# Layer 0's experts in order of their token counts, ten alone and six in pairs, rows fetched from DRAM

## Chip, cores and metric

One core of a Trainium2 chip (trn2). The metric is the device time of one execution in microseconds (us); smaller is better. All times are of this one core.

## What is computed

A two-layer block (mixer, then a mixture of experts, MoE) followed by a second block. Layer 0's mixer is a Fourier and neighbourhood attention mixer, layer 1's is retention. The change is in layer 0's MoE, which takes 512 tokens (256 of the context, 256 of the sequence) of 1024 numbers and 16 experts:

```python
def moe_ffn(tok, router_w, router_b, w1, w3, w2):
    T = tok.shape[0]
    scores = jax.nn.sigmoid((tok @ router_w).astype(jnp.float32))
    biased = (scores + router_b.astype(jnp.float32)).reshape(T, N_GROUPS, EXPERTS_PER_GROUP)
    group_score = lax.top_k(biased, TOP_K)[0].sum(axis=-1)
    g_sel = jnp.argmax(group_score, axis=-1)
    in_group = jnp.take_along_axis(biased, g_sel[:, None, None], axis=1)[:, 0]
    _, local = lax.top_k(in_group, TOP_K)
    expert_idx = g_sel[:, None] * EXPERTS_PER_GROUP + local
    w = jnp.take_along_axis(scores, expert_idx, axis=-1)
    w = w / jnp.sum(w, axis=-1, keepdims=True)
    gate = ...
    for e in range(N_EXPERTS):
        hid = jax.nn.silu(tok @ w1[e]) * (tok @ w3[e])
        out = out + gate[:, e:e + 1] * (hid @ w2[e])
```

Each token goes to two of four experts in one group. w1 and w3 of an expert are 1024 x 512, w2 is 512 x 1024, all float32: 6 MB per expert, 96 MB per layer. The kernel never computes all 512 tokens for an expert; it collects the tokens that chose it, up to 128 places.

## The kernel before, in words

**Engines.** PE multiplies, PEld loads its weights, DVE and ACT and POOL do elementwise work, SP issues the loads. Each takes its instructions in order. The program is written as if in sequence; a scheduler orders each engine's instructions before the run.

**Float32 products in three passes.** `unit` (L191) loads 1 MB of weights and splits it in two halves of 128 x 1024: ACT writes the high part `wh` (L202), DVE the rest `wl` (L205), and POOL every fourth `wl` where `pool_every=4`. The split tiles have four buffers each. `mm3` then makes three matmuls: high by high, low by high, high by low (L214 to L216).

**Layer 0, `moe` (L1044).** `route` (L944) normalizes the tokens, finds each token's experts and gates, and its `rows` writes the tokens' rows to SBUF as `nat`, a high and a low half. `places` numbers the tokens of each expert. A one-hot matrix `oh` (`choose`, L1086) says which token holds which place, and `gather` (L1110) multiplies it with both halves of `nat`: this gives `xe`, the tokens of two experts with features on partitions. The loop goes over the experts in their fixed order, two to a one-hot. For each: w1's product, `silu`, one gather step of the next two experts, w3's product, the product of both, another gather step, then w2 of the expert before (`second`), then four transposes of the hidden layer. `slots` (L1094) multiplies the one-hot with gates and token numbers, so that DVE can compute which DRAM row a place belongs to (L1097 to L1101).

`second` scales the result by the gate. Experts 0 to 13 add it to `fD` in DRAM by an indirect DMA on POOL's queue (L1149); experts 14 and 15 stay on the chip and are put back by a matmul with a one-hot `back` (L1155, L1156) after the loop, where `fD` is read as `comb` and added to the residual.

**Overflow.** `overflow` (L1443), called in the second expert, reads a count into registers and branches (L1466): if an expert has more than 128 tokens, a loop over all experts serves the rest. Every engine passes that branch.

**Buffers.** Weights rotate through three raw buffers of 1 MB and two more of `moe`; SP issues each load when its buffer is free. Each weight load of layer 0 has runs of 2 KB, since row `k*128+p` goes to partition `p`. Part of layer 1's adaLN product (`ada`, L395) is put between the steps of the start by `fill`.

**Layer 1, `moe_late` (L1217), 256 tokens.** Its experts 0 to 13 are ranked on the chip by their counts, and 14 and 15 stay first in place (`NS = 2`). Two of them alone, then seven pairs that share PE's 128 columns (L1374); weights are used in float32 as loaded, in runs of 8 KB (partition `p` holds rows `8p` to `8p+7`), from an expert number that SP reads into a register. `GROUPS` gives the ranks and the places of each group, `caps` the places of each rank, and a token beyond them is the overflow's.

Of the kernel before, what the change touches and what calls it, by code (L numbers as in the profile page):

```python
# [18 lines left out]
P = 128  # L19
# [20 lines left out]
GROUPS = (((15, 128),), ((14, 128),), ((0, 96), (13, 32)), ((1, 96), (12, 32)), ((2, 64), (11, 64)),  # L40
          ((3, 64), (10, 64)), ((4, 64), (9, 64)), ((5, 64), (8, 64)), ((6, 64), (7, 64)))
BATCHES = ((0, 1), (2, 3), (4, 5), (6, 7), (8,))
CAPS = [dict(x for g in GROUPS for x in g)[r] for r in range(16)]


def host_constants():
# [13 lines left out]
    r = np.zeros((P, 44), f)  # L60
# [5 lines left out]
    r[:, 28:44] = CAPS  # L66
# [60 lines left out]
class Kern:  # L127
# [63 lines left out]
    def unit(self, w, kc0, c0, nk=8, ncol=256, pool_every=0):  # L191

        nc = self.nc
        src = w[kc0 * P:(kc0 + nk) * P, c0:c0 + ncol].rearrange("(k p) c -> p k c", p=P)
        t = self.raw((P, nk, ncol), src)
# [136 lines left out]
    def setup_late(self, pool):  # L332
        nc, I, cp, V = self.nc, self.I, self.cp, self.nc.vector
        row = lambda ap, p=P: ap.rearrange("(r p) -> r p", p=p)
        cr = cp.tile([P, 44], F32, name="c_route")
        nc.sync.dma_start(out=cr, in_=I["c_route"])
        self.wg4 = cr[:, 0:4]
        self.down16, self.caps = cr[:, 4:20], cr[:, 28:44]
# [605 lines left out]
    def route(self, l, ss, rp, spread):  # L944
# [69 lines left out]
        nat = [rp.tile([P, NT, D], F32R, tag=f"nat{i}", name=self.name("nat")) for i in range(2)]  # L1014

        def rows():
            for k in range(KC):
# [12 lines left out]
                if spread:  # L1030
                    w = P // KC
                    dst = [x.rearrange("p t (m q) -> p t q m", m=KC)[:, :, w * k:w * k + w, :] for x in nat]
                    self.split_evac(dst, tp.rearrange("p t (q m) -> p t q m", m=KC))
                else:
                    parts = self.split_evac([x[:, :, k * P:(k + 1) * P] for x in nat], tp)
                    if k == HK[0] and self.holds:
                        self.holds[0] = parts
                    if k == HK[1] and self.holds:
                        self.holds[1:] = [parts]
# [4 lines left out]
    def moe(self, ss):  # L1044
        nc, I, V = self.nc, self.I, self.nc.vector
        l, n0, NT, N = 0, 0, 4, 512
        with ExitStack() as es:
# [4 lines left out]
            self.aside.append(self.ada(1, 0, lambda i: wp.tile([P, 2048], F32, tag=f"xe{i % 2}", name=self.name("ada"))))  # L1052
            self.fill(2)
            tl, places, gates, rows, nat = self.route(l, ss, rp, False)
            rows()
            pos, posm = places()
            cnt = tl([2])
            V.tensor_reduce(out=cnt[:, 0:1], in_=pos[:, 4, :], axis=AX.X, op=OP.max)
            g, den = gates()

            pk = tl([16, NT, 4])
            pe = pk.rearrange("p e t c -> p t e c")
            V.tensor_tensor(out=pe[:, :, :, 3], in0=g, in1=den, op=OP.mult)
            nc.gpsimd.tensor_copy(pe[:, :, :, 0], posm)
            for t in range(NT):
                nc.gpsimd.tensor_copy(pe[:, t, :, 1:3], self.tokm[:, t].unsqueeze(1).to_broadcast([P, 16, 2]))

            pr4 = tl([16, NT, 4], F32R)
            nc.gpsimd.tensor_copy(pr4[:, :, :, 0:3], pk[:, :, :, 1:4])
            nc.gpsimd.tensor_tensor(out=pr4[:, :, :, 3:4], in0=pk[:, :, :, 3:4], in1=pr4[:, :, :, 2:3].bitcast(F32),  # L1070
                                    op=OP.subtract)
            iota = tl([N], F32, "iota")
            nc.gpsimd.iota(iota, pattern=[[1, N]], base=0, channel_multiplier=0, allow_small_or_imprecise_dtypes=True)
            idx = tl([16], I32, "idx")
            fidx = tl([16])
            gate = tl([16])

            direct = range(14, 16)

            def choose(p):  # L1080


                oh = wp.tile([P, NT, 256], F32R, tag="oh", name=self.name("oh"))
                for t in range(NT):
                    for e in range(2):
                        V.tensor_scalar(out=oh[:, t, e * P:(e + 1) * P], in0=self.iota1,  # L1086
                                        scalar1=posm[:, t, 2 * p + e:2 * p + e + 1], scalar2=None, op0=OP.is_equal)
                return oh

            def slots(p, oh):  # L1090
                sp = self.psum((P, 2, 4))
                for e in range(2):
                    for t in range(NT):
                        nc.tensor.matmul(sp[:, e, :], oh[:, t, e * P:(e + 1) * P], pr4[:, 2 * p + e, t, :],  # L1094
                                         start=t == 0, stop=t == NT - 1)
                c = slice(2 * p, 2 * p + 2)
                V.tensor_reduce(out=gate[:, c], in_=sp[:, :, 2:4], axis=AX.X, op=OP.add)  # L1097
                V.tensor_scalar(out=fidx[:, c], in0=sp[:, :, 1], scalar1=-4096.0, scalar2=4096.0, op0=OP.mult, op1=OP.add)
                V.tensor_tensor(out=fidx[:, c], in0=fidx[:, c], in1=sp[:, :, 0], op=OP.add)
# [893 lines left out]
```

## Time and profile before

| | us |
|---|---|
| median of three runs | 1775.08 |
| lowest, highest | 1773.9, 1779.36 |
| the profiled execution: its own time | 1774.75 |
| the profiled execution: span of its trace | 1773.0 |

| engine | busy us in the span | share |
|---|---|---|
| PE | 1680.7 | 95% |
| DVE | 1028.8 | 58% |
| ACT | 778.6 | 44% |
| POOL | 372.9 | 21% |

The span runs from the first to the last instruction; the profiled execution's own time is 1.75 us longer. The shares are averages over stages with different limits. Matmuls overlap, so the sum of their busy times is more than their time; distances between starts are safer. A line number is that of the helper which records the instruction, so L205 stands for every split half in the program. "idle before, releaser" is the time an engine stood still ahead of a group of instructions and what ended it.

### The profile page before, as it was taken

The page shows a single profiled execution, that of the slowest core. Times are in us where ns is not written, and L with a number is a line of the kernel's source. Part 1 is how long each engine was busy: PE and PEld are TensorE (multiplying, and loading weights), DVE is VectorE, ACT ScalarE, POOL GpSimd, SP SyncE. Part 2 cuts the span into 40 slices and gives each one's busy share as a digit, 9 for nine tenths or more (in the row PEclk, how much of TensorE's full clock was granted, in tenths as well). Part 3 has the DMA queues.
Part 4 walks back from the last instruction along what each step waited for, and adds up shares of the span by engine and source line. Part 5 has one row for each costly group of instructions (what it writes and reads, how often), then busy time and mean ns, then how long its engine had stood idle before and what let it go on. Part 6 is the DMA issues. An engine that isn't in the chain of part 4 may idle for free. (4 is left out here: it accounts for less than half of the span.)

```text
span 1773.0 us, 27976 instructions
## 1 busy us (share of the span) xinstructions
PE 1680.7 (95%) x11244; PEld 1337.9 (75%) x11244; DVE 1028.8 (58%) x1718; ACT 778.6 (44%) x1146; POOL 372.9 (21%) x282
## 2 busy tenths in 40 slices
PE   5999999999999999899999989999998999999999
PEld 3776658677888887688899975444348999988899
DVE  6565563777888878845445442211126756677665
ACT  3343332566666666534334341111025555655543
POOL 2212101234444444122012020000003110123310
PEclk8999999899999999899999989999998999999999
DMA  9635552569989889535633467899985544533360
GB/s 315 161 110 168 195 186 96 221 238 301 293 293 291 294 287 327 202 126 193 201 124 100 130 219 247 348 415 420 420 338 162 181 135 157 174 120 119 120 214 25
DMA packets 212306, 384.04 MB, mean 217 GB/s; under 512 B 24273, under 2 KB 141074, under 8 KB 194698
## 3 DMA queue, kind: packets, MB, share of 16 engines
q1 hardware_dynamic: 208682, 373.72, 60.7%
q0 software_dynamic: 2608, 7.08, 1.9%
q8 instruction: 91, 1.49, 0.4%
q10 hardware_dynamic: 880, 1.38, 0.2%
q14 instruction: 45, 0.37, 0.1%
HBM read 375.20 MB, written 12.75 MB: 219 GB/s over the span
## 5 line engine op out<-in xcount | busy, mean ns | idle before, releaser
L205 DVE TENSOR_TENSOR wl<-w,wh 128x1024 fp32r<-128x1024 f32 x350 | 468.1, 1349 | 189.9 <-ACT wh L202 188.6
L202 ACT ACTIVATE wh<-w 128x1024 fp32r<-128x1024 f32 x400 | 419.5, 1058 | 276.5 <-PE ps L216 144.8
L205 POOL TENSOR_TENSOR wl<-w,wh 128x1024 fp32r<-128x1024 f32 x50 | 137.0, 2740 | 161.3 <-ACT wh L202 161.3
L214 PE MATMUL ps<-wh,xh 128*128 128x256 f32 x512 | 146.9, 287 | 2.3 <-DVE qk L552 1.6
L216 PE MATMUL ps<-wh,xl 128*128 128x256 f32 x512 | 145.0, 283 | 0.0
L215 PE MATMUL ps<-wl,xh 128*128 128x256 f32 x512 | 145.0, 283 | 0.0
L1374 PE MATMUL ps<-w,xe 128*64 128x512 f32 (+2 forms) x640 | 135.5, 595 | 0.0
L215 PE MATMUL ps<-wl,xe 128*128 128x512 f32 x256 | 102.8, 402 | 13.2 <-POOL wl L205 13.2
L214 PE MATMUL ps<-wh,xe 128*128 128x512 f32 x256 | 102.8, 401 | 2.4 <-PEq L1466 2.4
L214 PEld LDWEIGHTS ps<-wh,xh 128*128 128x128 f32 x512 | 98.2, 192 | 6.5 <-issue 3.4
L214 PE MATMUL ps<-x,wh 128*128 128x256 f32 x352 | 102.4, 291 | 0.0
L216 PE MATMUL ps<-wh,xe 128*128 128x512 f32 x256 | 101.7, 397 | 0.0
L1374 PEld LDWEIGHTS ps<-w,xe 128*64 128x64 f32 (+2 forms) x640 | 44.3, 131 | 74.4 <-issue 70.1
L215 PE MATMUL ps<-x,wh 128*128 128x256 f32 x352 | 99.9, 284 | 0.0
L216 PE MATMUL ps<-x,wl 128*128 128x256 f32 x352 | 99.9, 284 | 0.0
L215 PEld LDWEIGHTS ps<-wl,xh 128*128 128x128 f32 x512 | 98.3, 192 | 0.1
L216 PEld LDWEIGHTS ps<-wh,xl 128*128 128x128 f32 x512 | 98.2, 192 | 0.0
L214 PE MATMUL ps<-xh,wh 128*128 128x512 f32 (+1 forms) x224 | 82.4, 379 | 2.4 <-ACT xh L540 2.1
L215 PE MATMUL ps<-xl,wh 128*128 128x512 f32 (+1 forms) x224 | 82.3, 369 | 0.3 <-DVE xl L541 0.3
L216 PE MATMUL ps<-xh,wl 128*128 128x512 f32 (+1 forms) x224 | 81.2, 366 | 0.0
L563 ACT ACTIVATE p<-ps,st 128x512 f32<-128x512 f32 (+1 forms) x64 | 38.5, 605 | 76.0 <-DVE st L560 69.6
L1110 PEld LDWEIGHTS ps<-oh,nat 128*128 128x128 f32 x512 | 67.3, 195 | 4.5 <-DVE oh L1086 1.2
(459 smaller groups left out, 3973.2 us busy)
## 6 DMA issues: line engine op xcount, KB each, us to landing
w<-in_moe_w_dram SPq DMA_DIRECT2D x192, 1024.0 KB, 7.7
w<-in_w_in_dram SPq DMA_DIRECT2D x48, 1024.0 KB, 5.2
w<-in_ada_w_dram SPq DMA_DIRECT2D x32, 1024.0 KB, 4.9
w<-in_ret_w_in_dram SPq DMA_DIRECT2D x24, 1024.0 KB, 5.4
w<-in_mixab_w_in_dram SPq DMA_DIRECT2D x10, 1024.0 KB, 6.4
w<-in_ada_w_dram SPq DMA_DIRECT2D x16, 512.0 KB, 8.9
ada<-in_ada_w_dram SPq DMA_DIRECT2D x8, 1024.0 KB, 9.9
w<-in_ret_w_out_dram SPq DMA_DIRECT2D x8, 1024.0 KB, 5.0
```

The source lines that it names most:

```text
L202: nc.scalar.activation(hi, t[:, b:b + hk], AF.Copy)
L205: eng.tensor_tensor(out=lo, in0=t[:, b:b + hk], in1=hi.bitcast(F32), op=OP.subtract)
L214: mm(ps, lh, rh, start=start, stop=False, skip_group_check=skip)
L215: mm(ps, lh, rl, start=False, stop=False, skip_group_check=skip)
L216: mm(ps, ll, rh, start=False, stop=stop, skip_group_check=skip)
L563: nc.scalar.activation(p[:, 0:w], S, AF.Exp, bias=st[:, 0:1], scale=1.0, accum_out=st[:, 1:2])
L1110: nc.tensor.matmul(ps[:, j], nat[part][:, t, k * P:(k + 1) * P], oh[:, t], start=t == 0, stop=t == NT - 1)
L1374: nc.tensor.matmul(ps[a:b], lhs(u * m + k)[:, a:b], we[e][:, k, 512 * c:512 * c + 512], start=u == k == 0, stop=u == len(ws) - 1 and k == ...
```

## The change

Layer 0's MoE takes over layer 1's ranking, and has its own groups: experts 15 and 14, then the ranked ones, ranks 0 to 7 alone with 128 places, ranks 8 to 13 in three pairs with 64 places each. Experts alone still go through the three passes; pairs use float32 weights as loaded. The rows are one float32 tile `nat`, written to a DRAM tensor `xnD`; `fetch` computes the token numbers of a group and gets its rows by an indirect DMA into one of three tiles `xg`; `turn` transposes these on PE. Weights are loaded in runs of 8 KB, with 3 + 3 raw buffers. The adaLN part is filled in whole before the first product. The overflow's branch stands in the last group and is taken when a count is above its rank's places. Layer 1 calls the same helpers as before under new names.

```diff
+one, two = lambda r: ((r, 128),), lambda a, b: ((a, 64), (b, 64))
+GROUPS = ((one(15), one(14), one(0), one(1), two(8, 13), one(2), one(3), two(9, 12), one(4), one(5), two(10, 11),
+           one(6), one(7)),
+          (one(15), one(14), ((0, 96), (13, 32)), ((1, 96), (12, 32)), two(2, 11), two(3, 10), two(4, 9), two(5, 8),
+           two(6, 7)))
...
-        nat = [rp.tile([P, NT, D], F32R, tag=f"nat{i}", name=self.name("nat")) for i in range(2)]
+        nat = [rp.tile([P, NT, D], F32R if l else F32, tag=f"nat{i}", name=self.name("nat")) for i in range(1 + l)]
...
+                    if k % 2:
+                        last = V.tensor_copy(dst[0], tp)
+                    else:
+                        last = nc.scalar.activation(dst[0], tp, AF.Copy)
...
+            es.enter_context(self.buffers(3, side="right"))
             rp, wp = op("route"), op("moe", 2)
-            es.enter_context(self.buffers(2))
...
             rows()
+            self.xnD = self.tc.dram_tile([N, D], F32, name="xnD")
+            for t in range(NT):
+                nc.scalar.dma_start(out=self.xnD[t * P:(t + 1) * P, :], in_=nat[0][:, t])
+            self.fill(99)
...
+            def fetch(gi):
+                oh = wp.tile([P, NT, P], F32R, tag="oh", name=self.name("oh"))
...
+                sp = self.psum((P, 2, 4))
+                for i, (r, _) in enumerate(GR[gi]):
                     for t in range(NT):
+                        nc.tensor.matmul(sp[:, i], oh[:, t], pr4[r][:, r, t, :], start=t == 0, stop=t == NT - 1)
...
+                V.tensor_copy(idx[:, c], fidx[:, c])
...
+                nc.gpsimd.indirect_dma_start(
+                    out=xg[gi % 3], out_offset=None, in_=self.xnD[:, :],
+                    in_offset=bass.IndirectOffsetOnAxis(ap=idx.bitcast(U32)[:, c], axis=0),
+                    bounds_check=N - 1, oob_is_err=False)
...
+            def turn(gi, c):
...
+                for j in range(4):
+                    k = 4 * c + j
+                    self.T(tp[:, j, :], xg[gi % 3][:, k * P:(k + 1) * P])
...
+                if single:
+                    self.split_evac(dst, tp)
+                else:
+                    nc.scalar.activation(dst[0], tp, AF.Copy)
+            def product(outs, name, n, cols, x, gi):
+                m = 2048 // cols
+                for u in range(2):
+                    ts = [self.expert_load(l, order, name, r, u, n, cols) for r, _ in GR[gi]]
+                    if len(ts) == 1:
+                        hi, lo = self.parts(ts[0], m, cols, 4)
+                    for k in range(m):
...
+                            if len(ts) == 1:
+                                self.mm3(ps, (x[0][:, q], x[1][:, q]), (hi[k][:, s], lo[k][:, s]), first, last)
+                                continue
+                            for i, t in enumerate(ts):
+                                a = slice(64 * i, 64 * i + 64)
+                                nc.tensor.matmul(ps[a], x[0][:, q, a], t[:, k, s], start=first, stop=last)
...
+            fetch(0)
+            fetch(1)
+            pm, oi, ranked = self.ranking(tl, pos, NT, lambda: wp.tile([P, NT, 16, 16], F32, tag="y", name=self.name("rk")))
+            ranked(place, posm, V)
+            for c in range(2):
+                turn(0, c)
+            gr = tl([NT, 16])
+            ranked(gr, g, nc.gpsimd)
...
+            for gi in range(NG):
+                if gi >= NS:
+                    self.places_of(order, oi, GR[gi])
...
+                product([h1], "moe_w1", 8, 512, xs[gi], gi)
...
+                if gi + 1 < NG:
+                    turn(gi + 1, 0)
...
+                product([h3], "moe_w3", 8, 512, xs[gi], gi)
...
+                if gi + 1 < NG:
+                    turn(gi + 1, 1)
+                if gi + 2 < NG:
+                    fetch(gi + 2)
+                if gi:
+                    second(gi - 1, hid)
+                if gi == NG - 1:
...
+                    self.overflow(l, N, NT, cnt, pk, nat, None, hs[:, 0:1], room, wp)
...
+    def expert_load(self, l, order, name, r, u, n, c):
+        w = self.I[name][l]
+        w = w[r:r + 1] if r >= 16 - NS else w[bass.ds(order[r], 1)]
+        m = 2048 // c
+        return self.raw((P, m, c), w.rearrange("o (p k) c -> p (o k) c", k=n)[:, u * m:u * m + m, :])
...
-        with self.tc.If(reg > limit):
+        with self.tc.If(reg > 0):
```

A pair's result goes to `fD` with two indirect DMAs, one for each expert's places. The order that the scheduler makes of it is shown at two places, each engine's rows from top to bottom.

POOL, at the start of layer 0, before (`hn` are normalized rows, `r` the gates, `wl` the low halves of the weights):

```order
L1022 TENSOR_TENSOR hn_2919<-hT,r_2789 128x512
L1069 CAST r_2961<-r_2954 128x64x3
L1070 TENSOR_TENSOR r_2961<-r_2954,r_2961 128x64
L205 TENSOR_TENSOR wl_3119<-w_3112,wh_3118 128x1024
L205 TENSOR_TENSOR wl_3196<-w_3189,wh_3195 128x1024
```

and with the change (L1493 ranks the gates, `rk`):

```order
L1027 TENSOR_TENSOR hn_2917<-hT,r_2789 128x512
L1503 TENSOR_TENSOR r_3078<-r_3042,c_route 128x256
L1493 TENSOR_TENSOR rk_3068<-r_2977,r_3042 128x1024
L1120 DMA xg_2829<-xnD,idx_2986 128x1024
L1120 DMA xg_2830<-xnD,idx_2986 128x1024
L1089 CAST r_3071<-r_3067 128x4x16
L1508 TENSOR_TENSOR r_3082<-r_2975,r_3079 128x4x16
L210 TENSOR_TENSOR wl_3123<-w_3116,wh_3122 128x1024
```

The first two fetches now stand behind the ranking of the gates, and the first low half behind the fetches.

PE, in the first pair (the fifth group) with the change: the slot matmuls of the seventh group (`ps_3894`), the last products of the pair's w3 (L1159), the pair's hidden layer (`hp`), and the transposes of the seventh group's rows `xg_2829`, which lie on the fetch that these slots start:

```order
L1109 MATMUL ps_3894<-r_3071,oh_3889 128x4 x4
L1159 MATMUL ps_3855<-w_3870,xe_3673 64x512
L1159 MATMUL ps_3855<-w_3868,xe_3673 64x512
L1159 MATMUL ps_3855<-w_3870,xe_3673 64x512
L1159 MATMUL ps_3855<-w_3868,xe_3673 64x512
L1159 MATMUL ps_3855<-w_3870,xe_3673 64x512
L1159 MATMUL ps_3855<-w_3868,xe_3673 64x512
L1159 MATMUL ps_3855<-w_3870,xe_3673 64x512
L279 MATMUL ps_3960<-c_main,hp_3880 128x128 x4
L219 MATMUL ps_3908<-wh_3912,hh_3809 128x512
L219 MATMUL ps_3909<-wh_3912,hh_3809 128x512
L279 MATMUL ps_4019<-c_main,xg_2829 128x128 x4
```

Before, the rows of the next experts came from SBUF by matmuls, with no transfer between slots and products.

PE, in layer 0 before, in the first expert, where a gather step of the next two experts stands between w3's last products and the slots:

```order
L216 MATMUL ps_3166<-wh_3195,xe_2979 128x512
L1110 MATMUL ps_3212<-oh_3135,nat_2828 128x256 x8
L1110 MATMUL ps_3222<-oh_3135,nat_2829 128x256 x8
L1094 MATMUL ps_3232<-r_2961,oh_2969 128x4 x8
L274 MATMUL ps_3245<-c_main,hid_3088 128x128 x4
```

The two rows of L1110 are gone with the change; transposes of fetched rows (L279 with `xg`) stand in such places.

## Rows read from the trace of the kernel before

**Rows 1.** Busy time by stretch: us from span start, then engine busy (x count), clock, DMA.
```profile
core 0: us, PE busy (x) PEld busy (x) DVE busy (x) ACT busy (x) POOL busy (x), PEclk, DMA share, GB/s
313.90:344.90 31.00, 26.73 (x168) 17.86 (x169) 23.69 (x66) 19.31 (x34) 10.30 (x10) 0.75 0.49 187
344.90:395.90 51.00, 48.59 (x264) 38.79 (x262) 37.67 (x59) 30.15 (x33) 15.46 (x7) 0.98 0.75 256
443.90:579.50 135.60, 130.35 (x675) 108.93 (x674) 111.96 (x121) 90.89 (x103) 60.84 (x24) 1.00 0.90 288
...
690.00:737.00 47.00, 40.94 (x235) 30.06 (x233) 35.00 (x57) 24.58 (x33) 14.66 (x10) 0.95 0.85 308
1210.00:1300.00 90.00, 85.86 (x409) 35.99 (x404) 12.69 (x34) 8.47 (x14) 0.00 (x0) 1.00 1.01 420
```

**Rows 2.** Groups by line, 300 to 730 us: busy us, mean ns | idle before, releaser.
```profile
L205 POOL TENSOR_TENSOR wl<-w,wh 128x1024 fp32r<-128x1024 f32 x48 | 132.3, 2756 | 151.8 <-ACT wh L202 151.8
...
L214 PE MATMUL ps<-wh,xe 128*128 128x512 f32 x256 | 102.8, 401 | 2.4 <-PEq L1466 2.4
...
L1149 POOL DMA_INDIRECT fD<-y,idx x14 | 30.5, 2179 | 69.2 <-DVE r L1098 32.4 <-ACT wh L202 24.0 <-DVE r L1099 5.5
```

**Rows 3.** Timeline of ACT: the silu of the fifth and the eleventh expert.
```profile
443.85 0.60 ACT L1171 ACTIVATE hid<-ps 128x512 f32<-128x512 f32 x1 [1.37 <-PE ps L216]
...
579.45 0.60 ACT L1171 ACTIVATE hid<-ps 128x512 f32<-128x512 f32 x1 [1.39 <-PE ps L216]
```

**Rows 4.** Timeline of PE in the expert loop: start us, us, what.
```profile
377.95 2.07 PE L1110 MATMUL ps<-oh,nat 128*128 128x256 f32 x16
...
385.44 0.60 PE L274 MATMUL ps<-c_main,hid 128*128 128x128 f32 x4
385.80 1.03 PE L1094 MATMUL ps<-r,oh 128*128 128x4 f32 x8
...
695.19 0.40 PE L214 MATMUL ps<-wh,hh 128*128 128x512 f32 x1
...
700.81 0.60 PE L274 MATMUL ps<-c_main,hid 128*128 128x128 f32 x4
```

**Rows 5.** Waits, longest first, 443.9 to 579.5 us: total us, times, longest.
```profile
PE ps L215 <- POOL wl L205: 5.3, 6, 1.0
```

**Rows 6.** Timelines of DVE and POOL: split halves side by side, and an index chain.
```profile
342.16 1.22 DVE L205 TENSOR_TENSOR wl<-w,wh 128x1024 fp32r<-128x1024 f32 x1
...
343.89 2.83 DVE L205 TENSOR_TENSOR wl<-w,wh 128x1024 fp32r<-128x1024 f32 x1
...
343.10 2.54 POOL L205 TENSOR_TENSOR wl<-w,wh 128x1024 fp32r<-128x1024 f32 x1 [10.15 <-ACT wh L202]
...
482.28 0.16 DVE L1097 TENSOR_REDUCE r<-ps 128x2 f32<-128x4 f32 x1 [0.45 <-PE ps L1094]
...
487.52 0.15 DVE L1101 CAST idx<-r 128x2 int32<-128x2 f32 x1
```

**Rows 7.** Timeline of PE in layer 1, second products of a pair of experts.
```profile
1255.72 7.14 PE L1374 MATMUL ps<-w,hh 128*64 128x512 f32 x32
1262.83 0.50 PE L1380 MATMUL ps<-back,y 128*128 128x256 f32 x2
```

**Rows 8.** DMA queues and issues: 390 to 690 us, then the whole span.
```profile
q0 software_dynamic: 2006, 3.77, 8.2%
...
fD<-y,idx POOLq DMA_INDIRECT x14, 7.1
...
fD<-zero SPq DMA_DIRECT2D x4, 512.0 KB, 4.9
```

**Rows 9.** Start of layer 0: last rows, first product; layer 1: ranking on POOL.
```profile
337.38 1.49 DVE L554 TENSOR_TENSOR nat<-ps,nat 128x512 fp32r<-128x512 f32 x2 [1.23 <-ACT nat L551]
...
344.89 0.39 PE L214 MATMUL ps<-wh,xe 128*128 128x512 f32 x1
...
L1286 POOL TENSOR_TENSOR r<-r,r 128x512 f32<-128x512 f32 x1 | 1.3, 1262 | 0.9 <-DVE r L1316 0.9
```

More of the change, by code (lines that the diff above doesn't have):

```diff
@@ L1053, in moe @@
             self.fill(2)
-            tl, places, gates, rows, nat = self.route(l, ss, rp, False)
+            tl, places, gates, rows, nat = self.route(l, ss, rp)
+            xg = [tl([D], n="xg") for _ in range(3)]
+            for t in xg:
+                nc.gpsimd.memset(t, 0.0)
             rows()
+            self.xnD = self.tc.dram_tile([N, D], F32, name="xnD")
+            for t in range(NT):
+                nc.scalar.dma_start(out=self.xnD[t * P:(t + 1) * P, :], in_=nat[0][:, t])
+            self.fill(99)
@@ new lines, in moe @@
+            pr4 = {r: numbers(g) for r in (15,)}
+            pr4[14] = pr4[15]
+            def fetch(gi):
+                oh = wp.tile([P, NT, P], F32R, tag="oh", name=self.name("oh"))
+                a = 0
+                for r, n in GR[gi]:
+                    for t in range(NT):
+                        pl = (place if r < 16 - NS else posm)[:, t, r:r + 1]
+                        V.tensor_scalar(out=oh[:, t, a:a + n], in0=self.iota1[:, 0:n], scalar1=pl, scalar2=None,
+                                        op0=OP.is_equal)
+                    a += n
@@ L1194, in moe @@
+                hid = [wp.tile([P, 4, P], F32R if single else F32, tag=f"hh{i}", name=self.name("hh"))
+                       for i in range(1 + single)]
+                if single:
+                    self.split_evac(hid, tp)
+                else:
+                    nc.scalar.activation(hid[0], tp, AF.Copy)
             fn = rp.tile([P, NT, D], F32, tag="nat0", name="comb")
@@ L1241, in moe_late @@
             first = [loads(g) for g in range(NS)]
-            tl, places, gates, rows, nat = self.route(l, ss, rp, True)
+            tl, places, gates, rows, nat = self.route(l, ss, rp)
             self.holds = []
@@ L1391, in moe_late @@
                     if g >= NS:
-                        for r, _ in GROUPS[g]:
-                            order[r] = nc.values_load(oi[0:1, r:r + 1], engines=[mybir.EngineType.SP], min_val=0, max_val=15,
-                                                      skip_runtime_bounds_check_because="a place in a list of 16")
+                        self.places_of(order, oi, GR[g])
                     ws = loads(g) if g >= NS else first[g]
@@ L1441, in moe_late, with places_of @@
             return ss
-    def overflow(self, l, N, NT, cnt, limit, pk, wp, nat, acc, after):
+    def expert_load(self, l, order, name, r, u, n, c):
[3 more added lines that the diff above has]
+        return self.raw((P, m, c), w.rearrange("o (p k) c -> p (o k) c", k=n)[:, u * m:u * m + m, :])
+    def places_of(self, order, oi, group):
+        for r, _ in group:
+            order[r] = self.nc.values_load(oi[0:1, r:r + 1], engines=[mybir.EngineType.SP], min_val=0, max_val=15,
+                                           skip_runtime_bounds_check_because="a place in a list of 16")
@@ L1446, in overflow @@
+    def overflow(self, l, N, NT, cnt, pk, nat, acc, after, room, wp):
         nc, I, V = self.nc, self.I, self.nc.vector
```

339 lines of the change are left out of this document (154 added, 185 removed).

## The prediction

> **What bounds the kernel now.** I began with busy time by stretch [rows 1], because the change rewrites one stage, layer 0's mixture of experts, and leaves the rest alone. The stage has a start (313.9 to 344.9 us), a loop over sixteen experts (344.9 to 700.8) and an end (to 737). In the loop PE is busy for 130.4 of 135.6 us, DVE 112.0, ACT 90.9, POOL 60.8 (the third row of [rows 1]), so PE leads. The silu marks the experts: from the fifth to the eleventh are 135.6 us, 22.6 for each [rows 3].
>
> Since a matmul's busy time overlaps the next one's, I take PE's work from starts. Twenty-four products of a weight's high and low halves take 5.62 us (695.19 to 700.81 [rows 4]); an expert has three such sets, 16.9 us. The gathers of 16 matmuls take 2.07, two per expert 4.1. Four transposes take 0.36 and eight slot matmuls under 1.03, half of them per expert [rows 4]. That is 21.9 of 22.6 us; the rest is waiting, and what ends it is POOL's low halves [rows 5]. The other engines have slack of 4 us (DVE, 18.7 per expert) to 12 us (POOL, 10.1) [rows 1]. So an expert costs what PE does, and less work on PE is time gained, until DVE's 18.7 us is reached.
>
> **The sum, against the profiled execution (1774.75 us; the median of the runs is 0.3 more).**
>
> *Ten experts alone.* Each loses its two gathers (4.1 us) and gets eight transposes of fetched rows beside the four of its hidden layer: 16.9 + 3 x 0.36 + 0.5 = 18.5 us of PE. DVE and ACT keep almost the same list per expert (nine and twelve weight halves, two evictions, and so on), so 18.7 and 15.1 us [rows 1]; POOL gets a fetch of 2.18 [rows 2] on its 10.1. Three engines now stand near 18.5 where one did, with four split buffers between them. I take 20.5: the larger sum and nearly three times the 0.7 us that the loop loses now. The lower end is 18.7. The upper end comes from two halves split side by side: DVE's took 1.22 us alone and 2.83 beside POOL's, ending 1.1 us after it [rows 6]. Three more such surpluses of 1.6 give 23.5.
>
> The Trainium skill says why that end must be kept: SBUF — State Buffer, section "Who interferes with whom", has a DVE instruction with two SBUF inputs and a GpSimd instruction that reads SBUF exclude each other for the whole instruction. The 2.83 us agrees.
>
> *Three pairs.* Both experts' products in float32, 64 columns of the array each, run as in layer 1: one set of a pair took 7.1 us there [rows 7], three sets 21.4, with transposes and eight slot matmuls 23.5 us of PE. ACT and DVE split nothing. But a pair needs twelve loads of 1,048,576 bytes, and layer 1's pairs run at 420 GB/s with the queues full (the last row of [rows 1]): 30 us. A round of one pair and two single experts has 64.5 us of engine work (23.5 + 2 x 20.5) and 59.9 us of weight transfers. Beside these, fourteen scatters now hold 8.2% of 300 us [rows 8], 1.76 us each; a round has four, and three fetches that I put at the same, 12 us. Against that stands a lead of six buffers, 15 us, 5 per round: 67 us of transfers. I take 67 for a round. Lower end 64.5; upper end 78.6, were the rate the loop's present one (288 GB/s at a share of 0.90, so 320 [rows 1]).
>
> The Trainium skill gives about 358 GB/s between HBM and a core (SBUF — State Buffer, "A bandwidth-pool intuition that's wrong"); by it a round would be 70 us and 12 more. The 420 of the row decides.
>
> *The loop.* Four singles 82 and three rounds 201, less the last second product, which stands after the loop as it does now (5.6), and 3 for the overflow's branch, for which PE waits 2.4 us now [rows 2] and which moves from the second expert to the last group: 280.4 against 355.9 [rows 4, 9]. **75.5 us are gained.** With the reference's inputs the ranked experts hold 95, 92, 83, 75, 75, 72, 66, 65, 59, 57, 53, 50, 45 and 35 tokens, those left in place 61 and 41; all fit their places, so the branch isn't taken.
>
> *The start.* Now the gather reads SBUF, and the first product begins 6.0 us after DVE's last rows (338.9 [rows 9]). Without low halves the rows should end near 337. Then four writes to DRAM: about 2 us of issue and 4.9 to land [rows 8]. Meanwhile POOL's queue holds the ranking of the gates ahead of the first fetch; half as many elements took 1.26 us [rows 9], and it waits for DVE's ranking: about 345.5. The second fetch, which PE's order also puts ahead of the first product, is issued 2.2 later and lands after 7.1 (by the scatters [rows 8]); transposes and evictions end near 357: **12 us lost**. Ends: 351, and 368 if the six weight loads ahead in the queues are in the way (15 us). PE idles meanwhile, and the clock is 0.75 in this stretch already [rows 1], so full speed and half speed both occur: I put 3 us more, between none and 6. The adaLN part that moves ahead of the rows fills PE time that waits anyway; if the rows come later for it, the same is lost there.
>
> *The later fetches.* Each is asked for by slot matmuls and needed by transposes later in PE's order. Between lie DVE's index chain (5.2 us from first reduction to cast when POOL's split is in its way [rows 6]) and 7.1 us of fetch: 12.3. By the order and the prices above PE has 4 us of work there for the seventh group, 8.7 for the third, 11 to 13 for five others, 15 to 20 for four. The seventh waits 8.3, the third 3.6, the fourth and fifth 0.8 each: **14 us lost** (5 with a short chain, 25 with a long one). The groups fetched during a pair find DVE idle.
>
> *The rest.* Ranking on DVE (small instructions once) lies under the first fetch; the cover is the fetch's latency, counted. The end is unchanged: 0.
>
> Sum: -75.5 + 12 + 3 + 14 = -46.5, so **1728 us**; with the terms' nearer bounds 1710 to 1748.
>
> **Rivals.**
> *Engines closer to their sums.* Singles at 18.7 (-18) and no waits for fetches (-14): 1696. For it: buffers and queues have held PE at 97% before. Against: the index chain of [rows 6]. 14%.
> *POOL's splits block DVE* for whole instructions: 23.5 for a single, +30: 1758. For it: the 2.83 us; against: such halves are already part of DVE's 112.0 us in 135.6 [rows 1], and it keeps up. 12%. It is what the skill's rule quoted above would do.
> *Transfers bound the rounds* at 78.6: +35, 1763. For it: the loop's DMA share is 0.90 now; against: layer 1's 420 with the same shape of load. 6%.
> *Slower: fetches hold POOL's queue.* POOL takes instructions in order; a fetch whose index is late keeps the low halves behind it, and PE waits for these. DVE's 5.2 us for each of thirteen fetches is 68 us where 14 stand: 1782. It needs about 5.2 us per group to pass the present time and the bound of a measurement. For it: [rows 5] shows PE waiting for POOL; against: at most 1.0 us at once. 4%.
> *It doesn't do what it says:* a ninth-largest count above 64 would take the overflow's branch, 16 turns of 4 blocks of six loads, 958 us at 420 GB/s at least. With 59 it doesn't. 1%. And 3% that gains and losses cancel.
>
> **How the numbers follow.** My forecast has 60%. Of this kernel a measurement can tell about 0.3%, 5 us, from no change. Faster: 60 + 14 + 12 + 6 = 92%; within 0.3%: 3%; slower: 5%. The range takes the forecast's own 1710 to 1748, the blocked case, and most of the fast one: 1698 to 1760.
>
> **What would show it.** Silus of neighbouring singles some 20.5 us apart (18.7: first rival; 23.5: second); rounds of 67 us with about 400 GB/s; no gather matmuls; a first product near 357; PE waiting some 8 us for the fetch of the seventh group and 4 for the third; a branch without its body. The prediction is wrong if the loop is longer than 300 us or the first product later than 368.

## The result and the profile after

The changed kernel takes 1789.83 us in the median of seven runs (1783.46 to 1791.01), the kernel before 1773.9 in seven beside it (1773.01 to 1779.36): a ratio of 1.0077, 95% interval 1.0061 to 1.0093. It is slower by 0.8% where 1728 us were forecast. The profiled execution took 1789.83 us, its span 1788.1.

Three marks cut the span: PE's first product of layer 0, the last addition to the residual in layer 0, and the end. The forecast's column is made from the terms of its sum.

| us | before | forecast | after |
|---|---|---|---|
| first product at | 344.9 | 357 | 357.0 |
| from there to the end of layer 0 | 383.4 | 321.9 | 375.6 |
| behind layer 0 | 1044.7 | 1044.7 | 1055.5 |
| span | 1773.0 | 1726.5 (with 3 for the clock) | 1788.1 |

The start came out as forecast. The middle gained 7.8 us instead of 61.5, and behind layer 0 another 10.8 went. By the prediction's own marks the loop took 342.6 us, to the transposes of the last hidden layer at 699.6, where more than 300 was to be the sign of a wrong forecast. These are the stretches of the changed kernel that answer to [rows 1], from its first silu to its last and, within that, one round of a pair and two single experts:

```profile
365.63:686.41 320.78, 258.50 (x1106) 164.62 (x1106) 173.11 (x241) 136.54 (x162) 107.41 (x52) 0.93 0.85 305
514.99:602.47 87.48, 70.91 (x293) 42.37 (x293) 41.48 (x57) 32.49 (x39) 25.53 (x13) 0.91 0.85 311
```

PE had been busy for 96% of the loop [rows 1]; now it is busy for 81%. No other engine is near its limit, nor are the DMA engines (0.85). This round takes 87.5 us where 67 were forecast (the one ahead of it 91.3, the one behind it 83.9), and 16.6 of these PE stands still. The groups by line of the same loop, as in [rows 2], say what ended that (L220 is PE's low-by-high product, L210 the low half, L1192 the scatter, L279 the transposes):

```profile
L220 PE MATMUL ps<-wl,xe 128*128 128x512 f32 x143 | 62.3, 436 | 39.5 <-POOL wl L210 34.5 <-DVE wl L210 4.9
...
L1192 POOL DMA_INDIRECT fD<-y,half x6 | 10.6, 1760 | 44.9 <-DMA fD<-y,half 28.2 <-DVE y L1181 10.8 <-ACT wh L207 6.0
```

PE waited 34.5 us for low halves that POOL makes, against 13.8 in the whole loop before, 5.3 of them in the stretch of [rows 5]. POOL itself waited 28.2 us with the scatters of pairs, until `fD<-y,half`, another scatter of the same kind, had landed. Side by side in time, first POOL, then PE, behind the first pair:

```profile
497.19 1.99 POOL L1192 DMA_INDIRECT fD<-y,half  x1 [2.90 <-ACT wh L207]
508.47 1.56 POOL L1192 DMA_INDIRECT fD<-y,half  x1 [9.29 <-DMA fD<-y,half]
509.51 2.89 POOL L210 TENSOR_TENSOR wl<-w,wh 128x1024 fp32r<-128x1024 f32 x1
```

```profile
501.76 0.40 PE L219 MATMUL ps<-wh,xe 128*128 128x512 f32 x1
512.46 0.80 PE L220 MATMUL ps<-wl,xe 128*128 128x512 f32 x1 [10.30 <-POOL wl L210]
513.05 0.63 PE L221 MATMUL ps<-wh,xe 128*128 128x512 f32 x1
```

A pair ends in two scatters into one tensor. The second may not start before the first has landed, and POOL, which takes its queue in order, stands 9.3 us with it. The next low half is queued behind, so PE stands 10.3 us. The same happens at 599.9 us (9.3) and 683.9 us (10.0): 29.5 us in all. After the wait a matmul takes 0.63 us where it took 0.40. The granted clock has fallen from 2.4 to 1.2 GHz, here for 4.8 us:

```profile
512.46:517.30 4.84, 4.84 (x11) 3.79 (x12) 0.73 (x1) 2.31 (x3) 0.10 (x1) 0.50 0.83 290
```

### The profile page after: what moved, and what is told of

The parts are those of the page before. It is cut to its first block, busy times and chain, and to the rows that moved or that the text cites. A ratio compares the mean times of both kernels' runs of the same rounds, so it can differ in the third digit from the quotient of the medians.

```text
span 1788.1 us, 26831 instructions
## 1 busy us (share of the span) xinstructions
PE 1629.2 (91%) x10680; PEld 1239.9 (69%) x10680; DVE 941.9 (53%) x1703; ACT 693.4 (39%) x1055; POOL 346.2 (19%) x296
## 5 line engine op out<-in xcount | busy, mean ns | idle before, releaser
L210 DVE TENSOR_TENSOR wl<-w,wh 128x1024 fp32r<-128x1024 f32 x296 | 390.2, 1332 | 178.9 <-ACT wh L207 176.9
L207 ACT ACTIVATE wh<-w 128x1024 fp32r<-128x1024 f32 x328 | 340.5, 1056 | 233.6 <-PE ps L220 92.8
L220 PE MATMUL ps<-wl,xh 128*128 128x256 f32 x512 | 144.7, 283 | 0.0
L210 POOL TENSOR_TENSOR wl<-w,wh 128x1024 fp32r<-128x1024 f32 x32 | 85.8, 2681 | 134.5 <-ACT wh L207 134.4
L220 PE MATMUL ps<-wl,xe 128*128 128x512 f32 x160 | 70.0, 438 | 39.5 <-POOL wl L210 34.5
L220 PE MATMUL ps<-x,wh 128*128 128x256 f32 x352 | 99.7, 283 | 0.0
L220 PEld LDWEIGHTS ps<-wl,xh 128*128 128x128 f32 x512 | 98.1, 192 | 0.2
L220 PE MATMUL ps<-xl,wh 128*128 128x512 f32 (+1 forms) x224 | 84.1, 375 | 2.1 <-DVE xl L546 1.5
L220 PEld LDWEIGHTS ps<-wl,xe 128*128 128x128 f32 x160 | 32.9, 206 | 55.4 <-POOL wl L210 40.1
L219 PE MATMUL ps<-wh,xe 128*128 128x512 f32 x160 | 68.3, 427 | 2.6 <-ACT wh L207 2.6
L1388 PE MATMUL ps<-w,hh 128*64 128x512 f32 (+2 forms) x320 | 67.5, 607 | 0.7 <-ACTq L1535 0.7
L219 PEld LDWEIGHTS ps<-x,wh 128*128 128x128 f32 x352 | 67.1, 191 | 1.4
```

Of the source, the lines that this page charges most:

```text
L207: nc.scalar.activation(hi, t[:, b:b + hk], AF.Copy)
L210: eng.tensor_tensor(out=lo, in0=t[:, b:b + hk], in1=hi.bitcast(F32), op=OP.subtract)
L219: mm(ps, lh, rh, start=start, stop=False, skip_group_check=skip)
L220: mm(ps, lh, rl, start=False, stop=False, skip_group_check=skip)
L1388: nc.tensor.matmul(ps[a:b], lhs(u * m + k)[:, a:b], we[e][:, k, 512 * c:512 * c + 512], start=u == k == 0, stop=u == len(ws) - 1 and k == ...
```

## The experiments

**Theory A:** the second scatter's wait for the first on POOL's queue costs these 30 us and the clock behind them. **Rivals:** B, the fetches come late and PE waits for the transposes of their rows; C, the overflow's branch, now at the last group, holds back weights and the head of layer 1; D, DVE or the transfers are the bound and stalls only move. Twelve kernels were run, each beside the kernel before.

| | edit | us | ratio to before, 95% |
|---|---|---|---|
| 1 | second scatter later | 1757.28 | 0.9904 (0.9883 to 0.9926) |
| 2 | no low halves on POOL | 1758.21 | 0.9922 (0.9903 to 0.9941) |
| 3 | fetch a group earlier | 1777.88 | 1.0018 (1.0000 to 1.0037) |
| 4 | branch at the second group | 1796.5 | 1.0142 (1.0119 to 1.0164) |
| 5 | 1, and a third `half` | 1752.32 | 0.9877 (0.9846 to 0.9909) |
| 6 | 5 and 3 | 1740.62 | 0.9804 (0.9775 to 0.9833) |
| 7 | 6, ranking behind the fetch | 1741.57 | 0.9811 (0.9782 to 0.9840) |
| 8 | 2, 3 and a third `half` | 1727.66 | 0.9729 (0.9693 to 0.9764) |
| 9 | 8, other scratch for the branch | 1737.3 | 0.9788 (0.9760 to 0.9816) |
| 10 | 8, sixteen single groups | 1731.54 | 0.9765 (0.9734 to 0.9796) |
| 11 | before, no low halves on POOL | 1756.1 | 0.9890 (0.9868 to 0.9913) |
| 12 | 8, pairs one place sooner | 1723.98 | 0.9701 (0.9677 to 0.9725) |

**1, the second scatter a group later.** It is queued behind the low half of the next group's w3 (`low_on_pool` is the last low half given to POOL).

```diff
+                add(ix.pop(0), y)
+                if ix:
+                    late.append((ix[0], y))
...
+                while late:
+                    with self.tc.issue_after(self.low_on_pool.ins):
+                        add(*late.pop(0))
```

> The changed kernel with one edit: a pair's second scatter into the tensor of sums is queued on POOL one group later, behind the low halves of the next group's second weight, by which time the first has long landed. Theory A (the second scatter waits 9.0 to 9.9 us for the first to land, three times, and low halves stand behind it on POOL's queue): PE's three waits of 10.3, 9.3 and 10.0 us for a low half go, and with them 4 to 5 us at 1.2 GHz after each, about 2 us a time; 1789.8 - 29.6 - 6 = 1754, between 1750 and 1760. Rival B (late fetches set the pace): the time freed is lost again before the transposes of fetched rows, 1780 or more. Rival C (the overflow's branch at the last group, and the low clock after it): the first two waits' 20 us may go, the rest stays, 1766 to 1772.

1757.28: 32.5 us less, within theory A's bounds and outside both rivals'. The three waits are gone from the timeline of PE, but one of 7.2 us has come at 525.5 us:

```profile
525.51 0.79 PE L222 MATMUL ps<-wl,hh 128*128 128x512 f32 x1 [7.20 <-POOL wl L210]
```

POOL waited there 8.7 us with the fill of the third pair's `half`, the small tile that holds a pair's row numbers: a buffer that the first pair's second scatter still read. It is the same scatter, met through a buffer.

The size agrees in part by luck. Theory A has its gain in the middle; between the two profiled executions the middle became 25.0 us shorter and the stretch behind layer 0 another 9.3, while the first product came 3.0 later. Why the stretch behind layer 0 gained is not shown.

**2, no low halves on POOL.** Here the scatters stay side by side.

```diff
-                        hi, lo = self.parts(ts[0], m, cols, 4)
+                        hi, lo = self.parts(ts[0], m, cols, 0)
```

> The changed kernel with one edit: in layer 0 every low half is made by DVE, none by POOL; the scatters and their waits stay as they are. Theory A: POOL still waits about 9.5 us three times for a landing, but nothing that PE needs stands behind it, so the three waits of about 10 us on PE go; DVE takes over 28 halves at 1.3 to 2.7 us, 36 to 76 us more work in stretches where it was half idle, of which some 5 to 10 us shows; 1789.8 - 36 + 8 = 1762, between 1755 and 1770. Rival B (late fetches): 1780 to 1795. Rival D (DVE becomes the bound without POOL's share): 1790 or more.

1758.21: the same gain without touching a scatter. POOL still stands with each pair's second scatter, 9.5, 9.0 and 9.3 us, but PE waits for POOL no more:

```profile
516.21 1.57 POOL L1192 DMA_INDIRECT fD<-y,half  x1 [9.52 <-DMA fD<-y,half]
```

Experiments 1 and 2 take away the two ends of one chain, the wait and what is queued behind it, and either ends PE's three waits, as theory A says. The size of the gain is not the scatters' alone here: the edit also ends what POOL's halves cost apart from them (8 and 11 come back to that), and PE waits 18.0 us for fetched rows in the loop instead of 10.4. DVE's extra work showed up nowhere.

**3, rows fetched one group earlier.**

```diff
+            fetch(2)
...
-                if gi + 2 < NG:
-                    fetch(gi + 2)
+                if gi + 3 < NG:
+                    fetch(gi + 3)
```

> The changed kernel with one edit: each group's rows are fetched one group earlier (three groups ahead, the third right after the gates are ranked). Rival B: the waits of transposes for fetched rows inside the loop (4.7, 1.5 and 4.1 us) go and with them the low clock behind two of them, 1789.8 - 10.3 - 4 = 1775, between 1771 and 1782. Theory A: these waits go too, but the three of about 10 us behind the second scatter stay, so no more than those 10 us; if the stalls of about 10 us changed with the fetches, A would fall.

1777.88, 12 us less. PE's waits for fetched rows in the loop are gone, and its waits for POOL's halves stayed (36.0 us from 364 to 735 us, 35.7 without the edit). The late fetches are real, of about the size that the prediction gave them (14), and not the cause of the miss.

**4, the branch at the second group.**

```diff
-                if gi == NG - 1:
+                if gi == 1:
```

> The changed kernel with one edit: the overflow's branch (not taken) stands at the second group, as in the kernel before, instead of at the last. Rival C: the 3.1 us that PE's sequencer waits at the branch and the weak transfers around it (64 GB/s between 680 and 700 us) go, and layer 1's first weights come earlier, so that the stretch at 1.2 GHz behind layer 0 (732 to 763 us) shortens by up to 9 us; 1789.8 - 3 - 9 = 1778, between 1774 and 1786; what the branch costs at the second group, about 3 us, is in the upper end. Theory A: the three waits of about 10 us stay; no change within 4 us, 1786 to 1794.

1796.5, 6.7 us more, and above theory A's range too. As an account of the miss rival C falls, though behind layer 0 the span was 5 us shorter (1050.2): the second group now takes 41.5 us between silus instead of 25.2. Two waits at the branch (PEq is PE's own sequencer) and behind it are 6.4 of these 16.3 us:

```profile
404.78 0.77 PE L219 MATMUL ps<-wh,xe 128*128 128x512 f32 x1 [2.24 <-PEq L1535]
...
409.69 0.79 PE L220 MATMUL ps<-wl,xe 128*128 128x512 f32 x1 [4.14 <-DVE wl L210]
```

**5, a third `half`.** To experiment 1's kernel:

```diff
-                    half = wp.tile([P, 2], I32, tag="half", name=self.name("half"))
+                    half = wp.tile([P, 2], I32, tag="half", name=self.name("half"), bufs=3)
```

> The kernel of the late second scatter (first experiment) with one more edit: the small tile of indices `half` gets a third buffer. There PE still stood 7.2 us at the second round, where POOL waited 8.7 us with the fill of the third pair's `half` until the first pair's second scatter had landed and freed its buffer, low halves queued behind. Theory A: these 7.2 us go and about 2 us of low clock behind them, 1757 - 9 = 1748, between 1745 and 1752. Rival (that stall came from elsewhere, the transfers or DVE): 1755 to 1759.

1752.32, 5 us less than 1. The value is 0.3 us past what was expected, and the intervals of 1 and 5 overlap, so the runs alone do not settle the size. In its trace the wait of 7.2 us is gone: PE's waits for POOL's halves from 355 to 700 us are (total us, times, longest)

```profile
PE ps L222 <- POOL wl L210: 7.5, 11, 0.9
```

**6, both.** The edits of 5 and 3.

> The edits of the last one and the fetch one group earlier together. If the two kinds of wait lie one after the other, as the timelines have it, their gains add: 1748 - 12 = 1736, between 1732 and 1742. Rival: both only move PE up against the same next limit (the weights' transfers, about 70 us to a round of one pair and two single experts at 420 GB/s), so that little more than the larger gain is left, 1745 to 1750.

1740.62: the gains add. From the first product to the end of layer 0 it takes 335.6 us. 14 are still missing to the forecast's 321.9, which holds 14 more for late fetches that are gone here.

**7, the ranking of gates behind the first fetches.**

```diff
+            got = fetch(1)
...
+            with self.tc.issue_after(got.ins):
+                ranked(gr, g, nc.gpsimd)
```

(and the same around `beyond`)

> The edits of the last one, and POOL's two steps for the ranked gates and the limits (2.3 and 3.0 us) queued behind the first two fetches instead of ahead of them. The first fetch was issued at 350.6 us, 3 to 4 us after its rows had landed in DRAM (written from 340 to 342.3, 4.8 us to land); theory: the first product comes 3 us earlier, 1736 - 3 = 1733, between 1730 and 1737. Rival: the third group's fetch, which needs the ranked gates, now comes later and PE waits there what was gained, 1735 to 1742.

1741.57, no gain: the rival was right. PE got its first rows at 351.2 us, 2.7 sooner than in 6 (353.9), and waited 2.4 a little later for the ranked gates, which stand ahead of the first products in its order:

```profile
351.23 1.94 PE L281 MATMUL ps<-c_main,xg 128*128 128x128 f32 x8 [12.07 <-DMA xg<-xnD,idx]
...
356.23 1.01 PE L1111 MATMUL ps<-r,oh 128*128 128x4 f32 x4 [2.43 <-POOL r L1092]
```

**8, no low halves on POOL and the earlier fetch.** The edits of 2, 3 and the third `half`.

> The changed kernel with all low halves on DVE, the third buffer of `half` and the fetch one group earlier, the two scatters of a pair still side by side. Theory A: with nothing of PE's behind POOL's queue the order of the scatters costs nothing; 1758 - 12 = 1746, between 1738 and 1750. If it is as fast as the late second scatter with the earlier fetch (1732 to 1742), POOL's share of the low halves is worth nothing here; if DVE bounds it, 1755 or more.

1727.66, beyond every case that was written down: 13 us less than 6, in which POOL makes every fourth low half and the second scatter is late. POOL's share did not merely gain nothing, it seems to have cost. The scatter's place differs between 6 and 8 too; 11 changes POOL's share alone. The low halves of DVE from 365 to 660 us, in 6 and then in 8:

```profile
L210 DVE TENSOR_TENSOR wl<-w,wh 128x1024 fp32r<-128x1024 f32 x82 | 127.0, 1581 | 15.2 <-ACT wh L207 13.7 <-DVEq L1545 0.9
```

```profile
L210 DVE TENSOR_TENSOR wl<-w,wh 128x1024 fp32r<-128x1024 f32 x111 | 130.2, 1218 | 8.4 <-ACT wh L207 7.6 <-DVEq L1536 0.2
```

DVE makes 111 halves in the time in which it made 82 beside POOL. In 6 a half of DVE takes 1.23 us alone and 2.67 when POOL is in one, on DVE and then on POOL:

```profile
572.43 1.23 DVE L210 TENSOR_TENSOR wl<-w,wh 128x1024 fp32r<-128x1024 f32 x1 [2.09 <-ACT wh L207]
574.33 2.67 DVE L210 TENSOR_TENSOR wl<-w,wh 128x1024 fp32r<-128x1024 f32 x1 [0.67 <-ACT wh L207]
```

```profile
573.42 2.49 POOL L210 TENSOR_TENSOR wl<-w,wh 128x1024 fp32r<-128x1024 f32 x1 [5.30 <-ACT wh L207]
```

The Trainium skill's rule that the prediction quoted (SBUF — State Buffer, "Who interferes with whom") agrees with the 2.67 us. POOL's 28 halves in 6 take only 3 us off DVE's 130. PE's waits for low halves in 6, from 357.0 to 692.5 us, were

```profile
PE ps L222 <- POOL wl L210: 11.4, 14, 3.1
PE ps L222 <- DVE wl L210: 9.2, 10, 1.7
```

and in 8, which has no halves of POOL's, from 356.0 to 676.5 us:

```profile
PE ps L220 <- DVE wl L210: 2.8, 5, 0.8
```

One round of 8, and what its DMA queues moved in it (q1 the weights, q0 fetches and scatters):

```profile
485.05:556.87 71.82, 66.48 (x293) 39.72 (x292) 40.27 (x60) 32.20 (x40) 13.38 (x7) 1.00 0.98 373
```

```profile
q1 hardware_dynamic: 3414, 24.85, 86.8%
q0 software_dynamic: 961, 1.90, 11.4%
```

PE is busy for 66.5 us, near the forecast's 64.5 of engine work, but the DMA engines are the bound now, at 0.98: weights 62.3 us and the seven fetches and scatters 8.2.

**9, other scratch for the branch.** In 8, DVE waited 9.5 us ahead of the branch for the last pair's second scatter, since the branch's scratch tiles were `y` tiles; PE waited 7.1 behind it.

```diff
-                    room = (c4(t1("y", D)), t1("y", D), c4(m), t1("hh0", 512), c4(t1("hh1", 512)), None, t1("ovs", 64))
+                    room = (c4(xg[0]), xg[1], c4(m), t1("hh0", 512), c4(t1("hh1", 512)), None, t1("ovs", 64))
...
-                nc.sync.dma_start(out=fn[:, t, :], in_=self.fD[t * P:(t + 1) * P, :])
+                nc.gpsimd.dma_start(out=fn[:, t, :], in_=self.fD[t * P:(t + 1) * P, :])
```

> The eighth experiment's kernel (no low halves on POOL, fetch one group earlier) with two more edits: the overflow's branch takes two of the spent fetch tiles as scratch instead of the `y` tiles, and the four reads of the sums stand on POOL's queue instead of SP's. There DVE waited 9.5 us ahead of the branch until the last pair's second scatter had landed (its `y` tile was the scratch), PE 1.7 and 7.1 us behind it, and SP sent no weight between 619 and 638 us. Theory A (the same write after write, met a fourth time at the branch): 7.1 us of PE's wait go and the clock's fall behind it (about 2 us); 1727.7 - 9 = 1718.5, between 1713 and 1723. Rival (the end of layer 0 and the start of layer 1 are held by something else): 1725 to 1730.

1737.3, 10 us more, above both ranges. The wait at the branch went, as expected, but it had covered a longer one: the sums in `fD` can be read only when the same second scatter has landed, and now PE came there sooner and stood 12.3 us:

```profile
654.63 0.80 PE L1257 MATMUL ps<-c_main,comb 128*128 128x128 f32 x2 [12.25 <-DMA comb<-fD]
```

In 8 the sums' reads had been issued at 636 us, here at 646. Why the chain ended so much later is not settled: weights now flowed beside the scatters, the reads moved to POOL's queue, and two edits were made at once. And 4.7 us of the difference between the two profiled executions stand ahead of the first product (360.7 against 356.0), where neither edit acts; over the versions of the changed kernel that mark lies between 353.0 and 361.4, so single traces are not compared here for less than that.

**10, sixteen single groups.**

```diff
-GROUPS = ((one(15), one(14), one(0), one(1), two(8, 13), one(2), one(3), two(9, 12), one(4), one(5), two(10, 11),
-           one(6), one(7)),
+GROUPS = (tuple(one(r) for r in (15, 14, *range(14))),
```

> The eighth experiment's kernel with sixteen single groups in layer 0, no pairs. Theory T (with the stalls gone a round is bound by its weights: 71.8 us at 373 GB/s with the DMA engines busy 0.98, where PE is busy 66.5): a pair saves little, since two single experts take 2 x 18.7 us and a round of four would take 75 instead of 71; three rounds, + 12, 1740, between 1733 and 1748. Rival P (PE's sums count, as the prediction had it: a pair 23.5 us against two singles of 20.5): + 3 x 17.5, 1780 or more.

1731.54, just below theory T's range. Pairs are worth some 4 us, and the intervals of 8 and 10 overlap. Theory T's direction holds, rival P falls. Six single experts take 110.1 us between silus, 18.35 each, and three limits meet:

```profile
400.00:476.00 76.00, 76.00 (x370) 62.76 (x369) 74.97 (x111) 62.00 (x71) 15.54 (x8) 1.00 0.99 363
```

PE is busy throughout, DVE 75 of 76 us, the DMA engines 0.99. A pair takes work off PE and DVE but not a byte off the transfers.

**11, the kernel before without POOL's share.**

```diff
-                    hi, lo = self.unit(w, u, c0, 4, 512, pool_every=4)
+                    hi, lo = self.unit(w, u, c0, 4, 512, pool_every=0)
```

> The kernel before with one edit: layer 0's low halves all on DVE. Theory L (POOL's share of the low halves gains nothing since DVE's own take 2.6 us instead of 1.22 while POOL works on one): DVE's 182 halves at 1.22 are 222 us where 136 at 1.455 were 198, so DVE goes from 249 to 273 of 316 us and still fits, and the 13.2 us that PE waited for POOL's halves go; 1774 - 11 = 1763, between 1758 and 1772. Rival D (DVE is the bound there with all of them): 1778 or more.

1756.1, 18 us less, more than theory L gave. Low halves on DVE from 353.7 to 670 us, before and then here:

```profile
L205 DVE TENSOR_TENSOR wl<-w,wh 128x1024 fp32r<-128x1024 f32 x122 | 170.8, 1414 | 55.0 <-ACT wh L202 55.0
```

```profile
L205 DVE TENSOR_TENSOR wl<-w,wh 128x1024 fp32r<-128x1024 f32 x174 | 209.6, 1221 | 51.2 <-ACT wh L202 50.7
```

DVE makes 52 halves more for 39 us more, 0.75 us each. PE's waits in this stretch before, which are gone here:

```profile
PE ps L215 <- POOL wl L205: 11.7, 13, 1.6
```

So 18 us lay in the kernel before, apart from the change, and most of them were waits for POOL's own halves.

**12, each pair one place sooner.** From 8, so that three single groups follow the last pair.

```diff
+GROUPS = ((one(15), one(14), one(0), two(8, 13), one(1), one(2), two(9, 12), one(3), one(4), two(10, 11), one(5),
+           one(6), one(7)),
```

> The eighth experiment's kernel with each pair one place earlier in the order of groups, so that three single groups stand behind the last pair instead of two. Nothing is added or left out. Theory A (at the end of layer 0 the last pair's chain is exposed: first scatter, 9 to 10 us to its landing, second scatter, 8 to 10 us to its landing, and behind that the branch's scratch in one kernel and the reads of the sums in the other): with some 20 us more between that chain and the branch, DVE's 9.5 us and PE's 7.1 us at the branch go, and the reads of the sums find them landed; 1727.7 - 9 = 1718.5, between 1713 and 1723. Rival (layer 0's end is held by the transfers of the last weights, which come no sooner): 1725 to 1730.

1723.98, between theory A's range and the rival's: the fastest kernel here, 3% faster than before (2.75 to 3.23%), though not told apart from 8. DVE's wait ahead of the branch fell from 9.5 to 3.0 us and PE's behind it from 7.1 to none, with 2.9 left at the branch itself:

```profile
637.00 0.77 PE L219 MATMUL ps<-wh,xe 128*128 128x512 f32 x1 [2.89 <-PEq L1536]
```

The last silu came 5.5 us later than in 8 (631.4 against 625.9), 1.6 of that ahead of the first product; what the rest went on, I did not test.

## Why the prediction was wrong

**The step that failed** is in "Three pairs". It counted a pair's scatters as transfers ("fourteen scatters now hold 8.2% ... a round has four") and their places on POOL's queue at nothing. That the second writes where the first writes, and so waits for it to land, was costed nowhere. All it took was at hand: the landing time, 7.1 us [rows 8], and POOL's order in the changed program behind the first pair:

```
L1192 DMA fD<-y_4134,half_4137 512x1024 x2
L210 TENSOR_TENSOR wl_4189<-w_4182,wh_4188 128x1024
```

The Trainium skill (DMA: Bandwidth & Descriptors, "Rules for kernel authors") says why such a wait can't simply be left out: a DMA that accumulates reads its destination first and writes it later, and another write in between is lost. No run here shows that; every kernel kept the wait or moved it. Three times 7.1 would have been 21 us; measured are 29.5 us of PE's waits. With the clock and the buffer of `half`, experiments 1 and 5 took 30.2 us off the middle (375.6 to 345.4 between the profiled executions); the rest of their 37.5 us lies outside it.

The middle took 53.7 us more than forecast. By the traces 30.2 of these are this step's, 15.0 go from 6 to 8, where PE's waits for low halves fall from 20.6 to 2.8, and 12.7 remain in 8 (320.6 against 307.9, the forecast's middle without late fetches), 11 of them in its three rounds (212 us against 201). The late fetches give back 4.1: they cost 9.9 from 5 to 6, not 14. Each is a difference of single traces.

**The slower rival** had the place and the mechanism (a DMA that waits on POOL's queue keeps low halves behind it, and PE waits for these) but the wrong DMA: it blamed fetches with late indices, 5.2 us for each of thirteen. It was 9 to 10 us at each of three scatters. Its chance of 4% was argued from [rows 5], from a kernel that had no two scatters in a row.

**Singles at 20.5:** in the changed kernel the fourth single took 18.85 us between silus, where no late fetch or scatter was in the way, 18.35 in 10. The lower bound (18.7) was the right end: the surplus for three engines near their sums didn't come.

**Pairs and rounds:** the engine work was about right (64.5 in the sum, PE busy for 66.5 in a round of 8); the transfers were not 67 but 70.5 (62.3 and 8.2). The seven fetches and scatters cost 8 us, less than the 12 in the sum, but weights beside them ran at 399 GB/s by their share instead of 420, and the lead of six buffers, 5 us in the sum, does not show in a round (that it isn't won anew each time is argued, not measured). With the stalls gone the rounds of 8 take 69 to 72 us. The rate that the prediction set aside, the Trainium skill's 358 GB/s (SBUF — State Buffer, "A bandwidth-pool intuition that's wrong"), would have made the weights alone 70 us, and it is not the limit: 8 moved 417 GB/s from 507 to 532 us. Another page of the Trainium skill (HBM Reference, "Specifications (TRN2)") has a core that streams alone at about 425, which agrees.

**POOL's splits block DVE**, a rival with 12%, is true as a mechanism and was put at the wrong place. Taking POOL's halves away gained 13 us between 6 and 8 (which differ in the scatter's place too), and 18 us in the kernel before, where the prediction read them as part of DVE's busy time that "keeps up". DVE did keep up there, with 0.2 us of PE's waits; what PE waited for were POOL's own halves, 11.7 us there and 11.4 in 6, where DVE's took 9.2.

**Two rivals' sums** leave out that the prediction held its rounds at 67 by transfers. By its own terms singles at 18.7 would have gained 7 us and not 18, and singles at 23.5 cost 22.5 and not 30.

**The start** (first product at 357.0, forecast 357) is right in part by luck: the first fetch was issued at 350.6 us where the sum had about 345.5, and the first two landed in 4.4 where it had 7.1. **The later fetches** (12 us by experiment 3, forecast 14) were about right in sum; the seventh group waited 4.1 us instead of 8.3, the third 4.7 instead of 3.6. **Behind layer 0** the 0 was wrong: 10.8 us (the sum had 3 for the clock, at the start). In the head of layer 1 the clock stays at 1.2 GHz longer and PE stands idle for part of the time (busy times and granted clock in a stretch 10 us behind layer 0, before and then after):

```profile
738.30:743.30 5.00, 5.00 (x21) 4.49 (x20) 5.00 (x10) 2.87 (x5) 0.00 (x0) 0.60 0.01 2
743.30:748.30 5.00, 5.00 (x34) 4.49 (x33) 5.00 (x12) 4.40 (x9) 0.00 (x0) 1.00 0.02 3
```

```profile
742.50:747.50 5.00, 3.98 (x11) 2.63 (x12) 5.00 (x10) 4.88 (x8) 0.00 (x0) 0.50 0.00 0
747.50:752.50 5.00, 3.90 (x21) 3.46 (x20) 5.00 (x12) 3.55 (x7) 0.00 (x0) 0.77 0.00 0
```

The stretch behind layer 0 took between 1045.6 and 1055.7 us over the eleven versions of the changed kernel, 1046.2 of them in experiment 1, which left the branch where it was. Which of the load order, the branch and the clock sets it there was not taken apart, so this part of the miss stays open.

That 8 measures the forecast's 1728 is chance: it has neither the 14 us of late fetches that the sum contained nor POOL's halves.

## What to carry to other kernels

Before a step that issues two DMAs into one tensor goes on an engine's queue, ask whether the second waits for the first to land, and read in the program's order what stands behind it on that queue; the price is a landing time for each, paid by whoever needs the next instruction. When an engine shares work with another on the same memory, compare what both do with what one does alone: here a quarter of the halves on POOL took 3 us of 130 off DVE in 6 and, as an estimate, 25 of 196 in the kernel before (163 halves at the 1.2 us of 11), and both kernels were slower for it, since PE waited for the slower engine's halves. And when a step is cut on one engine, look for the next sum in the same stretch: pairs saved PE and DVE work that the transfers no longer let it use.

## What was not expected of the hardware

The changed kernel's fourteen scatters landed 9.6 us after their issue in the median (5.3 to 12.2), where those before took 7.1 [rows 8]. Half of a pair's rows are out of bounds in each scatter, and it does not reliably land sooner for that: over the changed kernel and its versions with pairs the medians in the loop were 8.1 to 11.0 us for such scatters and 7.4 to 10.4 for whole ones. And two engines splitting weights side by side finish hardly more than one: 82 halves by DVE and 28 by POOL in 127 us of DVE's time, 111 by DVE alone in 130.
